# Two of four counted V chunks in plain fp32, their gate rows fetched beside the fixed chunks, and a changed pace of the list

## The chip, the cores and the metric

One core of a Trainium2 chip runs the kernel. The metric is the time of one execution in microseconds (us) of the device, as the median of several runs. A profile is one further execution with the hardware profiler on; its span runs from the first instruction to the last.

## The reference

The kernel computes one encoder layer for 256 tokens of width 2048. Most of it (retention, a gated recurrence, cross attention) isn't touched. The change lies in the last part, a layer of 16384 single-neuron experts of which each token uses 128:

```python
def block(args):                     # xb: tokens, eb: their experts, gb: gates
    xb, eb, gb = args
    u = u_tab[eb]
    act = jax.nn.gelu(jnp.einsum('td,tkd->tk', xb, u).astype(jnp.float32))
    return jnp.einsum('tk,tkd->td', (gb * act).astype(xb.dtype), v_tab[eb])
```

So for each chosen expert there is a dot product with a row of U, a gelu, a gate, and a row of V added with that weight. The result is added to the residual stream and normed.

## The kernel before

**Three ways to an expert.** The experts are arranged in 128 columns of 128. Each way computes part of them.

- *Fixed columns.* The first 40 columns are computed for all 256 tokens, used or not, in five chunks (0 to 4) of eight columns. Their U and V are loaded densely with DMAs that SP issues, 512 KB each.
- *Counted columns.* The program counts which of the other columns are used most and takes 32 of them, chunks 5 to 8. Their U and V rows are gathered by index: one indirect DMA, issued by POOL, brings the 128 rows of a column (128 x 2048 numbers). Their gates come the same way, four indirect DMAs of 128 x 256 for half a chunk.
- *The list.* What then remains of a token's experts is worked off one by one: for each of up to 38 places of a token, in two blocks of 128 tokens, a row of U is gathered for every token of the block and multiplied with its activations (`dot`, L1415), later a row of V is gathered and added with its coefficient (`axpy`, L1423). Each is one DVE instruction over 128 x 2048 and one gather by POOL (L1408).

**Products.** A product of two fp32 operands is made in three parts. ACT rounds the weight tile to a high part (`hi`, L1350), DVE subtracts to get the rest (`lo`, L1369; L1366 where the tile comes from the transposer), and PE adds activation-high x hi, activation-low x hi and activation-high x lo (L1174 to L1177 in fixed, L1187 to L1190 in counted V chunks). A V step is one half megabyte of weights and twelve matmuls of 512 columns. The activations of a chunk are split the same way, by ACT (L1293) and DVE (L1297, tile `xe`). All eight sums of V live in eight PSUM banks.

**The order.** The stretch that the change touches is written out by hand. `run` (L1316) walks through a list of steps: 64 D steps (counted U; PE first transposes each half row tile, L1339), then the V chunks in the order 0, 1, 2, 3, 5, 6, 7, 8, sixteen steps each: W steps for fixed chunks, R steps for counted ones. Between them stand G steps, which load two halves of gates and multiply them into the next chunk's activations (L1274 for fixed chunks, L1285 for counted ones). Chunk 4 comes last, in `v_final`, after the loop. At step t the loop emits the high part of step t + 3, the low part of t + 2, loads of up to step t + 8 where a buffer is free, the matmuls of t, and then `wv.pump(rate)`. The pump lets the list go on: it adds the step's rate to a credit, and each list operation takes 2.2 from it. The rates are RU = 2.3 for a D step and RV = 1.35 for a V step. What is left of the list after the loop is emitted at once (`wv.drain`), ahead of `rest`, a branch that is skipped when the list was long enough, and of `v_final`.

**The buffers.** Weight loads and gates share six tiles (`spots`), two of which are the halves of the buffer that held chunk 0's activations. Row gathers of V take `rows_v`: the buffers that held the activations of chunks 1, 2, 3 and 5, each given when its activations have been split. The list has `ring`: four tiles, and from the sixth and seventh V chunk on one more each. `chosen` (L1442) refills it before each operation, with the buffer that the operation before has just used.

**The queues.** Each engine works off its instructions in the order of the program and waits at semaphores. POOL's queue is the one to watch: row gathers, gate gathers and list gathers stand in it in the order in which the loop emitted them, and where one waits for its buffer, all behind it wait too. SP issues only the dense loads here.

Of the kernel before, what the change touches and what calls it, by code (L numbers as in the profile page):

```python
# [18 lines left out]
P = 128  # L19
# [18 lines left out]
RG, RK, RU, RV = 8.0, 3.5, 2.3, 1.35  # L38
# [46 lines left out]
def hybrid_layer_kernel(ctx: ExitStack, tc: tile.TileContext, a: dict, out: bass.AP, dbg=None):  # L85
# [1105 lines left out]

    class Step:
        def __init__(self, kind, load, mms, rate, part=0, post=None):
            self.kind, self.load, self.mms, self.rate, self.part = kind, load, mms, rate, part
            self.post = post or {}
# [44 lines left out]
    def v_steps(i):  # L1240
# [17 lines left out]
        if i < NCH:  # L1258
            for dc in range(4):
                for q in range(4):  # L1260
                    yield Step("W", lambda b, dc=dc, q=q: nc.sync.dma_start(b, a["V"][i, dc, q]),
                               lambda hi, lo, dc=dc, q=q: products(hi, lo, dc, q), RV)
        else:
            for c in range(8):
                for half in range(2):
                    yield Step("R", None if half else column(c),
                               lambda hi, lo, c=c, half=half: r_mms(*ahs[i], hi, lo, c, half), RV, half)

    def prep_steps(i, gap=2):
# [40 lines left out]
        return reads, post  # L1310
# [6 lines left out]
    spots, rows_u, rows_v = [], [], []  # L1317

    def run(steps):
# [4 lines left out]
        def loads(limit):  # L1324
            for k, q in queues.items():
                while q and q[0] <= limit and free[k]:
# [16 lines left out]
        def high(t):  # L1343
            if t < len(steps) and steps[t].kind != "G":
# [10 lines left out]
        def low(t):  # L1355
            if t >= len(steps):
                return
# [14 lines left out]
            elif kind == "R" and steps[t].part:  # L1372
                rows_v.append(raws[t])
            del raws[t]
# [9 lines left out]
        for t, step in enumerate(steps):  # L1384
# [8 lines left out]
            if step.kind != "G":  # L1393
# [46 lines left out]
    def chosen():  # L1440
# [17 lines left out]
        held, taken = [], 0  # L1458
        for kind, tt, k, gs in ops:
# [17 lines left out]
            else:  # L1477
                while "v0" not in done:
                    yield 3.0
                axpy_pe(tt, k, mine[0])  # L1480
            ring.extend(mine)
            yield 0.4 if kind == "pe" else 2.2
# [235 lines left out]
    def begin():  # L1718
# [3 lines left out]
        spots.extend(held_in[ORDER[0]][:, 1024 * n:1024 * n + 1024] for n in range(2))  # L1722
# [8 lines left out]
    def given(n):  # L1731
        (rows_v if n < 5 else ring).append(held_in[ORDER[n]])
# [3 lines left out]
    attach(steps[-1], {1: [(begin, None)]})  # L1736
    for n, (i, nxt) in enumerate(zip(ORDER[:-1], ORDER[1:])):
# [5 lines left out]
        if n + 1 < NCH + NDY - 2:  # L1743
            attach(part[-1], {1: [(lambda n=n: given(n + 1), None)]})
        for k, g in enumerate(reads):
            part.insert(2 + 5 * k, g)
        steps += part
# [97 lines left out]
```

## Time and profile before

| what | value |
|---|---|
| median of 3 runs | 2057.37 us (2057.12 to 2061.39) |
| the profiled execution's own time | 2054.45 us |
| its span | 2052.7 us |
| mean granted TensorE clock | 0.966 |
| counted U stage | about 1255 to 1532 us |
| eight V chunks in the loop | about 1532 to 1980 us |
| chunk 4, norm and output | about 1980 to 2053 us |
| PE busy in the span | 1885.0 us (92%) |
| DVE busy | 1577.2 us (77%) |
| POOL busy | 547.7 us (27%) |

PE, DVE, ACT, POOL and SP are the engines; PEld is PE's loading of stationary operands. A row of a timeline gives the start, the duration, the engine, the line of the kernel, the operation, what it writes and reads, and in brackets how long its engine stood idle before it and what ended that. A POOL row is the issue of a gather, not the transfer. Busy time is no bound by itself: a stage is bound by what ends last there.

### The profile page before, as it was taken

The page shows a single profiled execution, that of the slowest core. Times are in us where ns is not written, and L with a number is a line of the kernel's source. Part 1 is how long each engine was busy: PE and PEld are TensorE (multiplying, and loading weights), DVE is VectorE, ACT ScalarE, POOL GpSimd, SP SyncE. Part 2 cuts the span into 40 slices and gives each one's busy share as a digit, 9 for nine tenths or more (in the row PEclk, how much of TensorE's full clock was granted, in tenths as well). Part 3 has the DMA queues.
Part 4 walks back from the last instruction along what each step waited for, and adds up shares of the span by engine and source line. Part 5 has one row for each costly group of instructions (what it writes and reads, how often), then busy time and mean ns, then how long its engine had stood idle before and what let it go on. Part 6 is the DMA issues. An engine that isn't in the chain of part 4 may idle for free. (4 is left out here: it accounts for less than half of the span.)

```text
span 2052.7 us, 27876 instructions
## 1 busy us (share of the span) xinstructions
PE 1885.0 (92%) x10196; PEld 1600.4 (78%) x10196; DVE 1577.2 (77%) x2402; ACT 916.2 (45%) x1418; POOL 547.7 (27%) x371
## 2 busy tenths in 40 slices
PE   9999999999999999999888787988999888877878
PEld 8888888888889888888777666877887766655666
DVE  6868967744566558999967576987999879866886
ACT  6566444544555545554556433333333332321333
POOL 1200000000000000000155312544634357868741
PEclk9999999999999999999999889999999999988989
DMA  8775656566655468556467876998988989797973
GB/s 291 264 224 172 213 162 192 162 197 191 186 173 146 154 185 292 168 180 201 147 136 153 213 241 241 394 355 304 390 328 316 416 334 348 261 359 287 365 273 129
DMA packets 203244, 499.87 MB, mean 244 GB/s; under 512 B 106760, under 2 KB 113032, under 8 KB 174856
## 3 DMA queue, kind: packets, MB, share of 16 engines
q1 hardware_dynamic: 72288, 254.23, 38.2%
q0 software_dynamic: 36240, 228.29, 28.7%
q10 hardware_dynamic: 94576, 15.54, 4.3%
q8 instruction: 80, 1.31, 0.3%
q14 instruction: 60, 0.49, 0.1%
HBM read 503.24 MB, written 21.30 MB: 256 GB/s over the span
## 5 line engine op out<-in xcount | busy, mean ns | idle before, releaser
L133 DVE TENSOR_TENSOR lo<-raw,hi 128x1024 fp32r<-128x1024 f32 x364 | 449.3, 1237 | 206.2 <-PE xc L187 125.2
L132 ACT CAST hi<-raw 128x1024 fp32r<-128x1024 f32 x364 | 382.0, 1052 | 288.8 <-PE xc L185 171.9
L142 PE MATMUL U<-xn,hi 128*128 128x512 f32 x1152 | 312.6, 407 | 0.4 <-DVE foldu L1221 0.4
L142 PEld LDWEIGHTS U<-xn,hi 128*128 128x128 f32 x1152 | 212.1, 194 | 37.1 <-DVE foldu L1221 0.7
L1415 DVE SCALAR_TENSOR_TENSOR junk<-at,h 128x2048 bf16<-128x2048 f32 x74 | 169.1, 2285 | 28.0 <-DMA at<-in_Us_dram,idx 27.9
L1350 ACT CAST hi<-kept 128x1024 fp32r<-128x1024 f32 x83 | 83.9, 1048 | 214.7 <-DMA kept<-in_Vs_dram,dyn 139.1
L144 PEld LDWEIGHTS U<-xn,lo 128*128 128x128 f32 x1152 | 158.5, 193 | 23.9 <-DVE lo L133 12.7
L144 PE MATMUL U<-xn,lo 128*128 128x256 f32 x1152 | 164.0, 285 | 9.7 <-DVE lo L133 9.7
L780 POOL DMA_DIRECT2D hn<-h x2 | 1.1, 566 | 508.6 <-DVE h L778 508.6
L1187 PE MATMUL acc<-hi,xe 128*128 128x512 f32 x256 | 107.5, 420 | 30.0 <-ACT hi L1350 30.0
L1423 DVE SCALAR_TENSOR_TENSOR hh<-at,coef,hh 128x2048 f32<-128x2048 f32 x47 | 110.2, 2346 | 29.5 <-DMA at<-in_Vs_dram,idx 29.5
L1369 DVE TENSOR_TENSOR lo<-kept,hi 128x1024 fp32r<-128x1024 f32 x83 | 99.7, 1218 | 33.4 <-ACT hi L1350 33.4
L1408 POOL DMA_INDIRECT at<-in_Us_dram,idx x74 | 82.7, 1117 | 139.1 <-DVE junk L1415 103.6
L142 PE MATMUL wb<-hT,hi 128*128 128x512 f32 x448 | 116.9, 396 | 0.0
L1113 POOL TENSOR_TENSOR kept<-kept 128x512 f32<-128x512 bf16 x64 | 77.3, 1216 | 122.8 <-DVE kept L1112 91.7
L1188 PE MATMUL acc<-hi,xe 128*128 128x512 f32 x256 | 106.3, 415 | 0.0
L1174 PE MATMUL acc<-hi,xe 128*128 128x512 f32 x240 | 97.9, 408 | 2.9 <-ACT hi L1350 2.8
L1408 POOL DMA_INDIRECT at<-in_Vs_dram,idx x47 | 82.2, 1749 | 57.5 <-DVE hh L1423 36.2
L1175 PE MATMUL acc<-hi,xe 128*128 128x512 f32 x240 | 96.1, 400 | 0.0
L1177 PE MATMUL acc<-lo,xe 128*128 128x512 f32 x240 | 67.5, 404 | 28.7 <-DVE lo L1369 16.2
L142 PEld LDWEIGHTS wb<-hT,hi 128*128 128x128 f32 x448 | 80.6, 189 | 13.9
L1112 DVE TENSOR_TENSOR kept<-kept,kept 128x512 bf16<-128x512 bf16 x128 | 69.8, 592 | 27.3 <-POOL kept L1113 15.2
(498 smaller groups left out, 4250.6 us busy)
## 6 DMA issues: line engine op xcount, KB each, us to landing
raw<-in_U_dram SPq DMA_DIRECT2D x80, 512.0 KB, 3.7
raw<-in_V_dram SPq DMA_DIRECT2D x61, 512.0 KB, 6.9
raw<-in_w_qkv_dram SPq DMA_DIRECT2D x48, 512.0 KB, 4.2
raw<-in_w_xyg_dram SPq DMA_DIRECT2D x44, 512.0 KB, 4.4
raw<-in_w_xk_dram SPq DMA_DIRECT2D x32, 512.0 KB, 3.6
raw<-in_w_xv_dram SPq DMA_DIRECT2D x32, 512.0 KB, 3.7
raw<-in_w_out_dram SPq DMA_DIRECT2D x32, 512.0 KB, 3.6
raw<-in_w_xq_dram SPq DMA_DIRECT2D x32, 512.0 KB, 3.6
```

The lines of the kernel that those rows point to most:

```text
L132: A.copy(hi, raw)
L133: V.tensor_tensor(lo, raw, hi.bitcast(F32), op=ALU.subtract)
L142: PE.matmul(pt, hi[:, ks], xt[:, kb, :], start=(kb == 0), stop=(kb == KB - 1))
L144: PE.matmul(pt[:, :T], lo[:, ks], xt[:, kb, :T], start=False, stop=False)
L1174: PE.matmul(pt, ah[:, c, t_], hi[:, w], start=(first and c == 0), stop=False)
L1175: PE.matmul(pt, al[:, c, t_], hi[:, w], start=False, stop=False)
L1187: PE.matmul(pt, ah[:, c, t_], hi[:, w], start=False, stop=False)
L1188: PE.matmul(pt, al[:, c, t_], hi[:, w], start=False, stop=False)
L1369: V.tensor_tensor(los[t], part_of(t), his[t].bitcast(F32), op=ALU.subtract)
L1408: G.indirect_dma_start(dst, None, src, bass.IndirectOffsetOnAxis(ap=ix, axis=0), bounds_check=n - 1, oob_is_err=False)
L1415: V.scalar_tensor_tensor(junk, gat, 1.0, h[0], op0=ALU.mult, op1=ALU.mult, accum_out=coef[tt][:, k:k + 1])
L1423: V.scalar_tensor_tensor(hh[tt], gat, coef[tt][:, k:k + 1], hh[tt], op0=ALU.mult, op1=ALU.add)
```

## The change

- Counted chunks 5 and 7 (`PLAIN`) are multiplied in plain fp32: four matmuls of fp32 operands a step in place of twelve, straight from the gathered rows and from the activations in their place. Their steps have no `hi` and no `lo`, and their activations are not split. A row buffer is handed back once PE's matmuls of the column are emitted, and the activations' buffer after the chunk.
- The G steps of all four counted chunks move into the four fixed chunks, two into each, at places 12 and 15. Those of the fixed chunks stay.
- A list operation's buffer goes back to the ring one operation later, from the end of the first V chunk on.
- The pump's rates become 1.9 for a D step, 1.25 for a split V step and 3.1 for a plain one.
- Row gathers may be loaded up to four steps earlier, and `rows_v` gets the buffers of chunks 1, 2, 3, 5 and 6, and at last the two halves of chunk 0's. The ring gets those of chunks 7 and 8.
- In `loads` the limit and the loop variable now share a name, so that one call takes at most one load from a queue.

```diff
-RG, RK, RU, RV = 8.0, 3.5, 2.3, 1.35
+RG, RK, RU, RV, RP = 8.0, 3.5, 1.9, 1.25, 3.1
+PLAIN = (5, 7)
...
+    def p_mms(av, row, c, half):
+        for tt in range(TT):
+            for d in range(2):
+                dc = 2 * half + d
+                PE.matmul(acc[dc][tt], av[:, c, tt * P:(tt + 1) * P], row[:, dc * 512:(dc + 1) * 512],
+                          start=False, stop=False)
...
-        if i < NCH:
+        if i in PLAIN:
+            for c in range(8):
+                for half in range(2):
+                    yield Step("R", None if half else column(c),
+                               lambda row, c=c, half=half: p_mms(acts[i], row, c, half), RP, half, plain=True)
+        elif i < NCH:
...
-        return reads, post
+        return reads, {} if i in PLAIN else post
...
-        def loads(limit):
+        def loads(t):
             for k, q in queues.items():
-                while q and q[0] <= limit and free[k]:
+                while q and q[0] <= t + (4 if k == "R" else 0) and free[k]:
                     t = q.pop(0)
...
+            if not queues["WG"] and lent and all(any(b is f for f in spots) for b in lent):
+                spots[:] = [f for f in spots if all(b is not f for b in lent)]
+                lent.clear()
+                rows_v.append(held_in[ORDER[0]])
...
-            if step.kind != "G":
+            if step.plain:
+                step.mms(raws[t])
+                if step.part:
+                    rows_v.append(raws[t])
+                del raws[t]
+            elif step.kind != "G":
                 step.mms(his.pop(t), los.pop(t))
...
-            ring.extend(mine)
-            yield 0.4 if kind == "pe" else 2.2
+            used.append(mine)
+            if len(used) > ("v0" in done):
+                ring.extend(used.pop(0))
+            yield 0.4 if kind == "pe" else 2.2
...
-        (rows_v if n < 5 else ring).append(held_in[ORDER[n]])
+        (rows_v if n < 6 else ring).append(held_in[ORDER[n]])
...
-        if n + 1 < NCH + NDY - 2:
-            attach(part[-1], {1: [(lambda n=n: given(n + 1), None)]})
-        for k, g in enumerate(reads):
+        for m in (n, n + 1):
+            if 0 < m < NCH + NDY - 1 and m == n + (ORDER[m] not in PLAIN):
+                attach(part[-1], {1: [(lambda m=m: given(m), None)]})
+        for k, g in enumerate(reads if nxt < NCH else []):
             part.insert(2 + 5 * k, g)
+        if n < len(early_reads):
+            for k, g in enumerate(early_reads[n]):
+                part.insert(12 + 3 * k, g)
```

POOL's queue at the start of the counted V chunks, before. `kept` tiles written from `in_Vs_dram,dyn` are V rows of a counted column, `at` and `h` tiles written from `in_Vs_dram,idx` are rows of the list, and `gt` is the table of gates (four gathers in the row marked x4).

```order
L1408 DMA h_4236<-in_Vs_dram,idx 128x2048
L1254 DMA kept_7753<-in_Vs_dram,dyn 128x2048
L1408 DMA at_10566<-in_Vs_dram,idx 128x2048
L1254 DMA kept_7754<-in_Vs_dram,dyn 128x2048
L1408 DMA at_10568<-in_Vs_dram,idx 128x2048
L1279 DMA raw<-gt,dyn 128x256 x4
L1408 DMA at_10570<-in_Vs_dram,idx 128x2048
L1254 DMA kept_7752<-in_Vs_dram,dyn 128x2048
```

The same place after the change (L1431 is the list's gather, L1263 the row's, L1293 the gates'):

```order
L1263 DMA kept_7752<-in_Vs_dram,dyn 128x2048
L1263 DMA kept_7753<-in_Vs_dram,dyn 128x2048
L1263 DMA kept_7754<-in_Vs_dram,dyn 128x2048
L1293 DMA kept_7751<-gt,dyn 128x256 x4
L1431 DMA at_10566<-in_Vs_dram,idx 128x2048
L1431 DMA h_4236<-in_Vs_dram,idx 128x2048
L1431 DMA at_10568<-in_Vs_dram,idx 128x2048
L1431 DMA at_10570<-in_Vs_dram,idx 128x2048
L1431 DMA at_10566<-in_Vs_dram,idx 128x2048
L1431 DMA h_4236<-in_Vs_dram,idx 128x2048
L1431 DMA at_10568<-in_Vs_dram,idx 128x2048
L1263 DMA kept_7752<-in_Vs_dram,dyn 128x2048
```

The last four gate gathers stand here, behind three row gathers and ahead of the first plain chunk. From there on no gate gather follows in POOL's queue, and two or three list gathers stand between two rows of a plain chunk, where there was one.

DVE's queue in the middle of the counted V chunks, before: `lo` is the low part of a half row tile, `hh` the list's sum.

```order
L1369 TENSOR_TENSOR lo<-kept_7753,hi 128x1024
L1423 SCALAR_TENSOR_TENSOR hh_14553<-at_10570,coef,hh_14553 128x2048
L1369 TENSOR_TENSOR lo<-kept_7753,hi 128x1024
L1369 TENSOR_TENSOR lo<-kept_7754,hi 128x1024 x2
L1423 SCALAR_TENSOR_TENSOR hh_14553<-h_4236,coef,hh_14553 128x2048
L1285 TENSOR_TENSOR kept_7750<-raw,kept_7750 128x1024
```

After the change, where chunk 6 ends and plain chunk 7 begins (L1446 is the list's operation, L1383 the low part):

```order
L1383 TENSOR_TENSOR lo<-kept_7754,hi 128x1024
L1446 SCALAR_TENSOR_TENSOR hh_14527<-at_10566,coef,hh_14527 128x2048
L1446 SCALAR_TENSOR_TENSOR hh_14527<-h_4236,coef,hh_14527 128x2048
L1446 SCALAR_TENSOR_TENSOR hh_14527<-at_10568,coef,hh_14527 128x2048
L1446 SCALAR_TENSOR_TENSOR hh_14527<-at_10570,coef,hh_14527 128x2048
```

In a plain chunk DVE has list operations one behind the other, 21 or 22 in each, and only the split of the next chunk's activations among them. In all, the order has 65 list operations in the U stage, 79 in the V chunks and 6 behind them before, and 54, 96 and none after; the four fixed chunks have 10 each before, and 10, 8, 9 and 10 after.

More of the change, by code (lines that the diff above doesn't have):

```diff
@@ L1190, in r_mms, with __init__ @@
                         PE.matmul(pt, ah[:, c, t_], lo[:, w], start=False, stop=False)
+    def p_mms(av, row, c, half):
[4 more added lines that the diff above has]
+                          start=False, stop=False)
     class Step:
-        def __init__(self, kind, load, mms, rate, part=0, post=None):
+        def __init__(self, kind, load, mms, rate, part=0, post=None, plain=False):
+            self.plain = plain
             self.kind, self.load, self.mms, self.rate, self.part = kind, load, mms, rate, part
@@ L1316, in hybrid_layer_kernel @@
     ahs, spare = {}, {}
-    spots, rows_u, rows_v = [], [], []
+    spots, rows_u, rows_v, lent = [], [], [], []
     def run(steps):
@@ L1343, in high @@
         def high(t):
-            if t < len(steps) and steps[t].kind != "G":
+            if t < len(steps) and steps[t].kind != "G" and not steps[t].plain:
                 his[t] = ws.tile([P, 1024], F32R, tag="hi", name="hi", bufs=4)
@@ L1355, in low @@
         def low(t):
-            if t >= len(steps):
+            if t >= len(steps) or steps[t].plain:
                 return
@@ L1457, in chosen @@
         gathers = [g for o in ops for g in o[3]]
-        held, taken = [], 0
+        held, taken, used = [], 0, []
         for kind, tt, k, gs in ops:
@@ L1480, in chosen @@
                 axpy_pe(tt, k, mine[0])
+            used.append(mine)
+            if len(used) > ("v0" in done):
+                ring.extend(used.pop(0))
+            yield 0.4 if kind == "pe" else 2.2
+        for mine in used:
             ring.extend(mine)
-            yield 0.4 if kind == "pe" else 2.2
         loose = [b for b in ring if all(b is not t for t in kept)]
@@ L1721, in begin @@
         ring.append(h[1])
-        spots.extend(held_in[ORDER[0]][:, 1024 * n:1024 * n + 1024] for n in range(2))
+        lent.extend(held_in[ORDER[0]][:, 1024 * n:1024 * n + 1024] for n in range(2))
+        spots.extend(lent)
     def after_first():
@@ L1736, in hybrid_layer_kernel @@
     attach(steps[-1], {1: [(begin, None)]})
+    early_reads = [prep_steps(i)[0] for i in ORDER if i >= NCH]
     for n, (i, nxt) in enumerate(zip(ORDER[:-1], ORDER[1:])):
```

## The prediction

> **What bounds the kernel now.** I read first the busy time by stage. The cuts are the counted U stage, the eight V chunks in their order (0, 1, 2, 3, 5, 6, 7, 8) and the closing part. The columns are start and end, length, busy time and count of PE, PEld, DVE, ACT and POOL, granted clock, DMA share, GB/s.
>
> ```profile
> 1255.00:1532.00 277.00, 247.36 (x1538) 216.45 (x1537) 236.97 (x301) 94.43 (x207) 135.81 (x99) 0.96 0.91 349
> 1532.00:1583.00 51.00, 46.94 (x197) 37.39 (x196) 47.92 (x47) 20.26 (x23) 21.09 (x13) 0.97 0.84 304
> 1583.00:1634.00 51.00, 45.79 (x194) 36.78 (x193) 45.03 (x34) 17.56 (x18) 18.36 (x11) 0.97 1.01 409
> 1634.00:1682.00 48.00, 45.51 (x193) 35.17 (x192) 43.76 (x30) 20.22 (x20) 22.77 (x9) 1.00 0.94 372
> 1682.00:1741.00 59.00, 47.57 (x195) 37.72 (x194) 47.20 (x32) 16.80 (x17) 44.12 (x24) 0.91 0.86 324
> 1741.00:1795.00 54.00, 47.50 (x195) 37.27 (x194) 44.80 (x31) 18.11 (x18) 43.97 (x25) 0.94 0.74 273
> 1795.00:1859.50 64.50, 50.86 (x193) 40.01 (x192) 45.00 (x30) 17.78 (x18) 45.92 (x25) 0.84 0.86 336
> 1859.50:1925.50 66.00, 49.74 (x192) 39.59 (x192) 45.79 (x31) 17.80 (x18) 49.87 (x28) 0.87 0.84 329
> 1925.50:1979.60 54.10, 48.44 (x200) 38.50 (x198) 47.07 (x31) 19.06 (x19) 35.82 (x19) 0.94 0.82 319
> 1979.60:2052.70 73.10, 51.50 (x200) 39.25 (x200) 48.63 (x55) 22.17 (x34) 18.73 (x12) 0.88 0.48 163
> ```
>
> DVE has the same 44 to 48 us of work in every V chunk, yet a chunk takes 48 to 66 us. What differs is POOL: 9 to 13 gathers in the three short chunks, 19 to 28 in the others. The timelines of POOL and DVE inside the sixth chunk show how the two are tied (start, duration, engine, line).
>
> ```profile
> 1820.31 0.99 POOL L1254 DMA_INDIRECT kept<-in_Vs_dram,dyn  x1 [0.30 <-issue]
> ...
> 1842.68 4.23 POOL L1408 DMA_INDIRECT kept<-in_Vs_dram,idx  x1 [0.30 <-issue]
> 1847.21 5.37 POOL L1408 DMA_INDIRECT at<-in_Vs_dram,idx  x1 [0.30 <-issue]
> ```
>
> ```profile
> 1827.21 2.35 DVE L1423 SCALAR_TENSOR_TENSOR hh<-at,coef,hh 128x2048 f32<-128x2048 f32 x1 [10.67 <-DMA at<-in_Vs_dram,idx]
> ...
> 1841.42 2.35 DVE L1423 SCALAR_TENSOR_TENSOR hh<-at,coef,hh 128x2048 f32<-128x2048 f32 x1
> 1843.69 1.22 DVE L1369 TENSOR_TENSOR lo<-kept,hi 128x1024 fp32r<-128x1024 f32 x1
> 1844.82 1.22 DVE L1297 TENSOR_TENSOR xe<-kept,xe 128x1024 fp32r<-128x1024 f32 x1
> 1845.96 2.35 DVE L1423 SCALAR_TENSOR_TENSOR hh<-at,coef,hh 128x2048 f32<-128x2048 f32 x1
> ```
>
> DVE sat idle for the 10.67 us before 1827.21, and there a gather is issued in 0.99 us. With DVE backlogged the one begun at 1842.68 ends at 1846.91, 0.95 us after the list operation of 1845.96 began. So a busy DVE lets about one gather through per list operation. A chunk has 10 list operations. In the fourth to eighth chunk POOL has 14 + 15 + 15 + 18 + 9 = 71 gathers more than that, and these chunks take 297.6 us, 72.6 us over five times 45: 1.02 us for each gather in excess. That price, PE's 2.72 us a step (below) and the DMA rate are what I cost the change with.
>
> **The change part by part.** The sum is against the profiled execution (span 2052.7 us, own time 2054.45 us); its result goes on the median of the runs, 2057.37 us, which is 2.9 us above that time.
>
> *U stage.* The starts of PE's transposes, then three DVE rows, show its pace:
>
> ```profile
> 1285.60 1.04 PE L1339 MATMUL uT<-ident,row 128*128 128x128 f32 x8
> 1289.26 1.04 PE L1339 MATMUL uT<-ident,row 128*128 128x128 f32 x8
> ...
> 1434.98 1.97 PE L1339 MATMUL uT<-ident,row 128*128 128x128 f32 x8 [5.86 <-DVE lo L1366]
> ...
> 1516.78 1.04 PE L1339 MATMUL uT<-ident,row 128*128 128x128 f32 x8
> ```
>
> ```profile
> 1375.88 1.28 DVE L1366 TENSOR_TENSOR lo<-uT,hi 128x512 fp32r<-128x512 f32 x2
> 1377.08 2.28 DVE L1415 SCALAR_TENSOR_TENSOR junk<-at,h 128x2048 bf16<-128x2048 f32 x1
> ...
> 1379.29 1.28 DVE L1366 TENSOR_TENSOR lo<-uT,hi 128x512 fp32r<-128x512 f32 x2
> ```
>
> PE needs 3.66 us a step. From 1285.60 to 1516.78 lie 55 steps, 201.3 us of work in 231.2: 30 us are lost to late rows. DVE needs 1.20 + 2.21 us a step, with 65 list operations on 64 steps, and half a fold besides: hardly less than PE, so it has no reserve to catch up with. The pump of 1.9 places 54 there: 11 x 2.21 = 24 us less DVE work, 0.38 us of reserve a step. I take 18 of the 30 us; the ends are 0 (late DMA alone sets it) and 28.
>
> *Fixed V chunks (first four).* All 32 gate-row gathers now stand here. The order gives 10 + 8 + 9 + 10 list operations and 8, 8, 8 and 11 gathers beyond them (the last with three row gathers), 35, where the table has 3 + 1 - 1 + 14 = 17. 18 x 1.02 = +18 us. DVE loses three list operations (6.8 us) and two residues (2.3 us), gains six gate products (6.8 us). The wait below goes, since the second chunk now has dot products only: -5.7.
>
> ```profile
> 1598.85 2.35 DVE L1423 SCALAR_TENSOR_TENSOR hh<-h,coef,hh 128x2048 f32<-128x2048 f32 x1 [5.70 <-DMA hh<-hd]
> ```
>
> Together +10 us. Ends: -8 if DVE's gaps take all extra gathers; +25 if each of the other three chunks pays the 11 us by which the fourth now exceeds the third (33 in place of 18). The loader now takes at most one weight load a step; I cost that at nothing, since each load waits for the buffer of the load six before it in either order, and SP has little else; without that cover every load would come two steps later.
>
> *Plain chunks (5 and 7).* On PE, twelve matmuls become four. The chain of waits has two fp32 products of 512 columns (four records), and PE's timeline the step of twelve:
>
> ```profile
> 2003.81 1.72 PE acc L1616 x4
> ```
>
> ```profile
> 1913.50 1.07 PE L1190 MATMUL acc<-lo,xe 128*128 128x512 f32 x4
> 1916.22 1.07 PE L1190 MATMUL acc<-lo,xe 128*128 128x512 f32 x4
> ```
>
> 4 x 0.86 = 3.44 us against 2.72: +11.5 us of PE a chunk, 55 instead of 43.5. DVE loses 16 subtractions of 1.13 us, but the pump of 3.1 puts 22 list operations there: 22 x 2.27 = 50 us. ACT's casts go, off the path. DMA carries 8 row gathers and 22 list gathers, costed from these:
>
> ```profile
> q0 software_dynamic: 11713, 71.94, 77.4%
> ...
> kept<-in_Vs_dram,dyn POOLq DMA_INDIRECT x31
> at<-in_Vs_dram,idx POOLq DMA_INDIRECT x25
> raw<-gt,dyn POOLq DMA_INDIRECT x12
> kept<-in_Vs_dram,idx POOLq DMA_INDIRECT x10
> h<-in_Vs_dram,idx POOLq DMA_INDIRECT x8
> kept<-gt,dyn POOLq DMA_INDIRECT x8
> ```
>
> ```profile
> 1600.00:1650.00 50.00, 45.38 (x191) 36.78 (x192) 49.79 (x34) 18.73 (x18) 24.86 (x11) 0.97 1.02 415
> ```
>
> A full row gather is 128 x 8 KB = 1.05 MB, a gate gather 0.13 MB; 71.94 - 31 x 1.05 - 20 x 0.13 leaves 36.8 MB for 43 list gathers, 0.86 MB each (rows out of bounds aren't fetched). 8 x 1.05 + 22 x 0.86 = 27.3 MB, at 415 GB/s 66 us. So DMA ends last and a plain chunk takes 66 us; the ends are 57 (PE alone) and 86 (second rival). A row's buffer now comes back when PE has done its column, not when DVE has split it: POOL waits there with up to three list gathers behind, up to 6.9 us, hidden while the ring holds rows.
>
> *Chunks 6 and 8.* Their gate gathers are gone, part of their rows comes early through six row buffers. Chunk 6: DVE 16 x 1.13 + 9 x 2.27 = 38.6 and 9 gathers in excess, 47.5 us. Chunk 8, in which the list ends: 18.1 + 7 x 2.27 + 4 x 1.13 + 6 = 44.5, say 45. With the plain ones 224.5 us against 54 + 64.5 + 66 + 54.1 = 238.6: -14. Ends -36 (57 + 44 + 57 + 44) and +26.
>
> *Hand-back one operation later* costs nothing: a gather still waits for the same operation four before it, and only lets other gathers pass in POOL's queue.
>
> *The end of the list.* Six list operations now follow the last step, and PE waits for them:
>
> ```profile
> 1992.01 2.07 PE L1177 MATMUL acc<-lo,xe 128*128 128x512 f32 x4 [12.48 <-DVE lo L1590]
> ```
>
> The new order has none; a branch and a first split stay, 2.5 us: -10 (ends -6, -12.5).
>
> Sum: -18 + 10 - 14 - 10 = -32 us; 2057.4 - 32 = 2025, I say 2026 us.
>
> A rule that speaks against the middle term: the Trainium skill, "SBUF — State Buffer", section "Who interferes with whom", says that a VectorE instruction with two SBUF inputs disturbs GpSimd only where that reads SBUF, and infers that descriptor generation escapes. The trace disagrees: 0.99 us against 4.23 and 5.37 under just such instructions.
>
> **The rivals.** *POOL is not the bound.* If the gathers in excess cost nothing and the long chunks waited for DMA, the fixed chunks gain 8 us instead of losing 10, and the others come to 66 + 44 + 66 + 44 = 220, -18: -18 - 8 - 18 - 10 = -54, 2003 us. For it: in the second chunk DMA runs at 409 GB/s. Against it: the seventh is longest at 329. That page's rule would give this case.
>
> *The list starves in the plain chunks* (the slower side). Four buffers serve 22 operations there, and lists stand before the next chunk's splits on DVE. A V load lands in 10.4 us in the fixed chunks, and with list operations back to back a gather took 2.98 us to issue:
>
> ```profile
> raw<-in_V_dram SPq DMA_DIRECT2D x40, 512.0 KB, 10.4
> ```
>
> ```profile
> 1977.65 2.98 POOL L1408 DMA_INDIRECT at<-in_Vs_dram,spi  x1 [1.67 <-DVE hh L1423]
> ```
>
> (2.35 + 2.98 + 10.4) / 4 = 3.9 us an operation, 86 us a plain chunk, the four 264.5, +26: sum +8, 2065 us. It decides from 82 us a plain chunk on, a landing of 9.6 us. Against it: fewer loads are in flight there.
>
> *Given back*: late DMA alone sets the U stage (0) and the fixed chunks pay the full +25; 0 + 25 - 14 - 10 = +1, 2058 us, no change. For it: the U stage runs at 349 GB/s with a DMA share of 0.91.
>
> **How the numbers follow.** Forecast (2026, its own ends 2010 to 2042) 0.54; POOL free (2003) 0.15; list starves (2065) 0.2; given back (2058) 0.11. About 0.2%, 4 us, can be told from no change. The given-back case is worth about that much to either side: 0.08 of its chance is the same, 0.01 faster and 0.02 slower, and 0.02 of the list case ends within 4 us. So faster 0.54 + 0.15 + 0.01 = 0.7, same 0.1, slower 0.2. The range leaves out the outer half of the two extreme cases: 1998 to 2064.
>
> **What would show it.** Right: U steps near 3.66 us with under 15 us lost; the fixed chunks 215 to 225 us with POOL at 17 or more gathers; 60 to 72 us for each plain chunk at about 400 GB/s, PE issuing 3.44 us steps; no 12 us gap ahead of L1617. Wrong: a plain step far from 3.44 us, plain chunks over 80 us, fixed chunks at 200, or U still losing 30 us.

## The result and the profile after

The changed kernel takes 2038.35 us (median of 4 runs, 2037.77 to 2039.42), the kernel before 2058.97 us beside it (4 runs, 2057.12 to 2061.39). The ratio is 0.990, with a 95% interval of 0.9883 to 0.9917. The profiled execution took 2037.77 us, its span is 2036.0 us. So the time fell by some 20 us where 31 were forecast; against the profiled execution before, by 16.7 us.

The busy time by stage of the changed kernel, cut at PE's first transpose of the U stage and at the first matmul of each V chunk (0, 1, 2, 3, 5, 6, 7, 8, then the closing part). The columns are those of the table in the prediction.

```profile
1260.60:1508.20 247.60, 238.96 (x1537) 214.57 (x1538) 213.97 (x277) 92.71 (x201) 119.77 (x89) 0.99 0.91 348
1508.20:1559.30 51.10, 46.78 (x194) 36.74 (x193) 45.86 (x44) 19.65 (x23) 30.35 (x20) 0.97 1.00 394
1559.30:1616.50 57.20, 47.92 (x194) 37.56 (x193) 46.48 (x42) 18.64 (x19) 27.69 (x17) 0.91 0.88 326
1616.50:1667.20 50.70, 46.03 (x194) 36.87 (x193) 45.57 (x38) 19.69 (x20) 30.94 (x17) 0.97 0.88 321
1667.20:1723.10 55.90, 46.70 (x194) 37.83 (x193) 41.60 (x27) 14.75 (x14) 33.63 (x22) 0.91 1.00 397
1723.10:1785.90 62.80, 55.92 (x130) 23.95 (x128) 46.96 (x21) 2.19 (x3) 47.31 (x26) 1.00 0.93 355
1785.90:1848.30 62.40, 50.17 (x193) 39.23 (x194) 46.17 (x28) 16.11 (x16) 42.77 (x25) 0.86 0.87 334
1848.30:1902.80 54.50, 54.50 (x130) 24.17 (x128) 36.03 (x16) 3.04 (x3) 32.59 (x20) 1.00 0.99 388
1902.80:1976.10 73.30, 51.04 (x194) 39.95 (x193) 55.49 (x39) 23.21 (x24) 34.52 (x21) 0.84 0.78 295
1976.10:2036.00 59.90, 50.75 (x209) 38.90 (x207) 36.79 (x48) 21.49 (x34) 9.67 (x7) 0.95 0.39 134
```

To compare every kernel by the same cuts, the next table gives the stage lengths in us, read from each one's profiled execution at the starts of the same instructions. "Fixed" is the sum of chunks 0 to 3. The last column is the median of the runs; the time before in the three sets of runs was 2057.2 (first four kernels of the experiments), 2057.9 (next four) and 2059.1 (last four). One far longer run each of rows_before (2613 us), ring6 (4766 us) and the kernel before (6455 us, second set) is in these medians and in none of the ratios; without it they are 2036.92, 2030.43 and 2056.84 us.

| kernel | U | fixed | 5 | 6 | 7 | 8 | closing | median |
|---|---|---|---|---|---|---|---|---|
| before | 275.9 | 208.5 | 53.7 | 64.7 | 66.2 | 52.3 | 75.1 | 2058.97 |
| changed | 247.6 | 214.9 | 62.8 | 62.4 | 54.5 | 73.3 | 59.9 | 2038.35 |
| rows_before | 268.1 | 200.7 | 56.0 | 65.3 | 63.8 | 52.0 | 74.4 | 2038.74 |
| dve_before | 257.7 | 186.0 | 51.1 | 52.2 | 51.9 | 43.9 | 70.6 | 1977.28 |
| rows_after | 245.8 | 207.7 | 58.0 | 60.7 | 54.5 | 66.6 | 59.9 | 2015.29 |
| dve_after | 243.6 | 203.3 | 59.3 | 58.2 | 54.5 | 62.7 | 59.9 | 2003.75 |
| no_plain | 246.5 | 247.5 | 56.2 | 59.7 | 55.2 | 57.8 | 61.6 | 2045.62 |
| gates_back | 248.4 | 203.5 | 74.8 | 66.5 | 60.0 | 77.2 | 59.9 | 2046.09 |
| loads_limit | 249.1 | 219.5 | 65.6 | 61.8 | 54.5 | 70.4 | 59.9 | 2042.24 |
| gates_earlier | 247.7 | 219.3 | 62.4 | 62.4 | 54.5 | 75.9 | 59.9 | 2038.83 |
| ring6 | 247.4 | 219.1 | 61.4 | 59.9 | 59.4 | 58.1 | 59.9 | 2030.98 |
| handback_now | 246.7 | 216.1 | 63.9 | 53.4 | 54.5 | 72.2 | 59.9 | 2030.83 |
| even_pace | 247.2 | 236.2 | 54.5 | 61.9 | 54.5 | 60.4 | 61.5 | 2034.34 |
| ring6_even | 248.8 | 228.1 | 56.6 | 56.0 | 58.1 | 53.9 | 59.9 | 2025.63 |

By these cuts the change did this: U -28.3, fixed chunks +6.4, counted chunks 236.9 to 253.0, so +16.1, closing part -15.2. The U stage begins 4.2 us later than before (1260.6 against 1256.4), though nothing ahead of it was touched; in the profiles of the other kernels it begins between 1257.5 and 1261.0, so this is spread between executions. The sum is -16.8, to 0.1 the difference of the spans. Each length comes from one execution. How far such lengths scatter can be read from ring6: in chunks 0 to 3 it has the same instructions in the same order as the changed kernel, and took 219.1 us for 214.9. So a difference of some 4 us in that column tells nothing by itself.

**U stage.** The same 55 steps as in the prediction, from PE's transposes of the ninth step to those of the last, take 208.91 us. With 201.3 us of work in them 7.6 us are lost, where 29.9 were.

```profile
1284.44 1.03 PE L1353 MATMUL uT<-ident,row 128*128 128x128 f32 x8
...
1493.35 1.04 PE L1353 MATMUL uT<-ident,row 128*128 128x128 f32 x8
```

So 22.3 of the 28.3 us come from these steps. Another 5.4 come from the eight steps ahead of them (23.85 us in place of 29.24), which the prediction's count of lost time left out.

**The plain chunks and what follows them.** PE's timeline (a bracket shows idle time and what ended it) in the plain chunks and at the start of chunk 8:

```profile
1723.08 41.66 PE L1197 MATMUL acc<-kept,kept 128*128 128x512 f32 x96
...
1894.60 8.75 PE L1197 MATMUL acc<-kept,kept 128*128 128x512 f32 x20
...
1920.69 2.08 PE L1191 MATMUL acc<-lo,xe 128*128 128x512 f32 x4 [15.52 <-DVE lo L1383]
```

Eight records make a step: 41.66 / 12 = 3.47 us. PE runs through chunk 7 in 54.5 us without one stop. Then it stands for 15.52 us at the first low part of chunk 8. DVE's timeline over that time:

```profile
1905.49 1.22 DVE L1311 TENSOR_TENSOR xe<-kept,xe 128x1024 fp32r<-128x1024 f32 x1
1906.95 2.35 DVE L1446 SCALAR_TENSOR_TENSOR hh<-h,coef,hh 128x2048 f32<-128x2048 f32 x1 [0.24 <-DMA h<-in_Vs_dram,idx]
1911.92 2.35 DVE L1446 SCALAR_TENSOR_TENSOR hh<-at,coef,hh 128x2048 f32<-128x2048 f32 x1 [2.62 <-DMA at<-in_Vs_dram,idx]
1914.77 4.74 DVE L1446 SCALAR_TENSOR_TENSOR hh<-at,coef,hh 128x2048 f32<-128x2048 f32 x2 [0.49 <-DMA at<-in_Vs_dram,idx]
1919.42 1.22 DVE L1383 TENSOR_TENSOR lo<-kept,hi 128x1024 fp32r<-128x1024 f32 x1
```

DVE is still on list operations that were placed in chunk 7, and waits for their rows. Of the 43 placed in the two plain chunks, 19 begin in chunk 5 and 15 in chunk 7. The low part needs none of them; it only stands behind them. In DVE's timeline 18 intervals in chunk 5 last 3.24 us each, 14 in chunk 7 3.68 us, against 2.27 us of work.

Chunk 6 doesn't begin so. Behind chunk 5 PE stops for 3.86 us for the first high part, then for 1.10 us for the first low part. The one long stop of chunk 6, 7.64 us, begins some 30 us into it and has another cause (handback_now, below).

**Closing part.** It has no list operation before PE's work, and PE has no gap ahead of L1617. The chain of waits there names the other direction, DVE waiting for PE:

```profile
DVE lo L1617 <- PE acc L1178: 6.3, 3, 3.3
```

### The profile page after: what moved, and what is told of

The parts are those of the page before. It is cut to its first block, busy times and chain, and to the rows that moved or that the text cites. A ratio compares the mean times of both kernels' runs of the same rounds, so it can differ in the third digit from the quotient of the medians.

```text
span 2036.0 us, 27487 instructions
## 1 busy us (share of the span) xinstructions
PE 1895.3 (93%) x10068; PEld 1574.0 (77%) x10068; DVE 1539.9 (76%) x2366; ACT 882.8 (43%) x1382; POOL 520.8 (26%) x371
## 4 chain that ended last, share of the span: by engine, by line
PE 51%; DMA 15%; issue 12%; DVE 12%; POOL 6%; ACT 2%; ACTq 1%; POOLq 0%; SPq 0%; DVEq 0%
PE wb L143 10%; PE xc L186 6%; PE xc L185 6%; PE xc L188 6%; PE wb L145 5%; DMA at<-in_Us_dram,idx 4%; DMA at<-in_Vs_dram,idx 3%; DVE lo L134 3%; POOL at L1431 3%; PE U L143 3%; PE U L145 1%; DMA h<-in_Vs_dram,idx 1%; PE G L1127 1%; DMA gt<-gs 1%; PE acc L1178 1%
## 5 line engine op out<-in xcount | busy, mean ns | idle before, releaser
L1438 DVE SCALAR_TENSOR_TENSOR junk<-at,h 128x2048 bf16<-128x2048 f32 x71 | 162.3, 2286 | 19.3 <-DMA at<-in_Us_dram,idx 19.3
L1446 DVE SCALAR_TENSOR_TENSOR hh<-at,coef,hh 128x2048 f32<-128x2048 f32 x54 | 127.0, 2351 | 45.4 <-DMA at<-in_Vs_dram,idx 43.8
L1364 ACT CAST hi<-kept 128x1024 fp32r<-128x1024 f32 x52 | 53.6, 1050 | 220.5 <-DMA kept<-in_Vs_dram,dyn 138.2
L1431 POOL DMA_INDIRECT at<-in_Us_dram,idx x71 | 83.9, 1181 | 132.4 <-DVE junk L1438 100.9
L1197 PE MATMUL acc<-kept,kept 128*128 128x512 f32 x256 | 111.0, 594 | 3.0 <-DMA kept<-in_Vs_dram,dyn 3.0
L1431 POOL DMA_INDIRECT at<-in_Vs_dram,idx x54 | 100.1, 1854 | 48.9 <-DVE hh L1446 26.9
L1175 PE MATMUL acc<-hi,xe 128*128 128x512 f32 x240 | 97.4, 406 | 6.6 <-ACT hi L1364 6.6
L1197 PEld LDWEIGHTS acc<-kept,kept 128*128 128x128 f32 x256 | 48.5, 190 | 64.4 <-issue 58.5
L1176 PE MATMUL acc<-hi,xe 128*128 128x512 f32 x240 | 95.9, 400 | 0.0
L1127 PE MATMUL G<-kept,kept 128*128 128x128 f32 x512 | 73.8, 296 | 18.6 <-POOL kept L1114 10.2
L143 PE MATMUL wb<-xT,hi 128*128 128x512 f32 x352 | 89.8, 397 | 0.0
```

The costliest lines, as they stand in the source:

```text
L143: PE.matmul(pt, hi[:, ks], xt[:, kb, :], start=(kb == 0), stop=(kb == KB - 1))
L1175: PE.matmul(pt, ah[:, c, t_], hi[:, w], start=(first and c == 0), stop=False)
L1197: PE.matmul(acc[dc][tt], av[:, c, tt * P:(tt + 1) * P], row[:, dc * 512:(dc + 1) * 512], start=False, stop=False)
L1431: G.indirect_dma_start(dst, None, src, bass.IndirectOffsetOnAxis(ap=ix, axis=0), bounds_check=n - 1, oob_is_err=False)
L1438: V.scalar_tensor_tensor(junk, gat, 1.0, h[0], op0=ALU.mult, op1=ALU.mult, accum_out=coef[tt][:, k:k + 1])
L1446: V.scalar_tensor_tensor(hh[tt], gat, coef[tt][:, k:k + 1], hh[tt], op0=ALU.mult, op1=ALU.add)
```

## The experiments

The first question was what holds the list back: the bytes of its gathers, or DVE's operations with POOL's issue beside them. Two edits answer it, each made to the kernel before and to the changed one.

### Fewer rows fetched: rows_before, rows_after

```diff
-                             bounds_check=n - 1, oob_is_err=False)
+                             bounds_check=(n * 5 // 8 if n == NS else n) - 1, oob_is_err=False)
         return dst
```

> The kernel before, with a lower bound for the list's gathers: rows in the last three eighths of the U and V tables are not fetched, so that a list gather moves about 0.54 MB in place of 0.86 (this changes the result; the number of gathers and all DVE work stay). If the counted U stage is bound by DMA, its 96 MB become about 75 MB and the stage falls from 276 us to the floor of PE, 245 to 255 us; if DVE's reserve is what it lacks, as the prediction had it, the stage stays at 268 to 278 us. For the V chunks with many gathers (59, 54, 65 and 66 us): POOL as the bound says unchanged within 3 us each, DMA as the bound says 8 to 15 us less in each.

> The changed kernel with the same lower bound for the list's gathers (0.54 MB in place of 0.86; this changes the result). The two plain chunks with the split chunk behind each took 125 and 128 us. If DMA sets the pace of the list there, the 85 MB of the four chunks become about 67 and they take 200 to 215 us in all; if the turn of POOL's issue and DVE's operation sets it, they take 240 to 253 us, and PE's first wait in the last of them stays over 10 us.

### Half the width on DVE: dve_before, dve_after

```diff
-        V.scalar_tensor_tensor(junk, gat, 1.0, h[0], op0=ALU.mult, op1=ALU.mult, accum_out=coef[tt][:, k:k + 1])
+        V.scalar_tensor_tensor(junk[:, :1024], gat[:, :1024], 1.0, h[0][:, :1024], op0=ALU.mult, op1=ALU.mult,
+                               accum_out=coef[tt][:, k:k + 1])
...
-        V.scalar_tensor_tensor(hh[tt], gat, coef[tt][:, k:k + 1], hh[tt], op0=ALU.mult, op1=ALU.add)
+        V.scalar_tensor_tensor(hh[tt][:, :1024], gat[:, :1024], coef[tt][:, k:k + 1], hh[tt][:, :1024],
+                               op0=ALU.mult, op1=ALU.add)
```

> The kernel before, with every list operation on DVE over 1024 of its 2048 columns (1.2 us in place of 2.35; this leaves out half of the list's sums); all gathers stay whole. If DVE lacks reserve in the counted U stage, it falls from 276 us to 245 to 255 us; if DMA bounds it, it stays at 268 to 278 us. In the long V chunks, POOL waiting for a busy DVE says that each falls to 47 to 50 us; DMA says that they stay within 4 us.

> The changed kernel with every list operation over 1024 of its 2048 columns (this leaves out half of the list's sums); all gathers stay whole. If DVE's operations and POOL's issue beside them set the pace of the list in the plain chunks, the four counted chunks fall from 253 us to 205 to 220; if DMA sets it, they stay at 240 us or more.

The U stage and the two longest V chunks (6 and 7) of rows_before, then of dve_before, in the columns of the stage table:

```profile
1258.50:1526.60 268.10, 246.22 (x1537) 218.03 (x1538) 236.49 (x300) 94.33 (x206) 137.31 (x99) 0.96 0.85 298
1783.20:1848.50 65.30, 49.05 (x193) 37.48 (x193) 44.98 (x31) 17.90 (x18) 51.75 (x28) 0.92 0.77 293
1848.50:1912.30 63.80, 49.81 (x194) 39.30 (x193) 45.91 (x31) 17.80 (x18) 49.80 (x28) 0.87 0.76 288
```

```profile
1260.20:1517.90 257.70, 240.43 (x1537) 215.11 (x1538) 177.48 (x307) 97.78 (x208) 113.69 (x101) 0.97 0.96 380
1754.90:1807.10 52.20, 46.26 (x193) 37.45 (x192) 35.58 (x31) 16.39 (x17) 34.44 (x27) 0.93 1.00 407
1807.10:1859.00 51.90, 45.71 (x194) 37.05 (x194) 35.53 (x31) 17.81 (x18) 37.83 (x25) 0.93 1.00 409
```

*U stage before:* 7.8 us go with fewer bytes, 18.2 us with half of DVE's list work. Neither alone gets what the change got, which took away 11 operations, bytes and DVE work together: 28.3. The two edits aren't equally strong. Fewer rows took 17% of the stage's bytes away (rate times length: 79.9 MB in place of 96.8), the half width took 25% of DVE's busy time (177.5 us in place of 236.7). *Long V chunks before:* fewer bytes change chunks 6 and 7 by +0.6 and -2.4 us, half of DVE's work by -12.5 and -14.3. So DMA was not their bound. Over the whole kernel before, half-width operations are worth 80 us (ratio 0.9613, 0.9561 to 0.9664).

*Counted chunks after the change:* 253.0 fall to 239.8 with fewer rows and to 234.7 with half of DVE's work. Each helps by 13 to 18 us, and neither clears the stage. The interval in the two plain chunks falls from 3.24 and 3.68 us to no less than 3.05 to 3.26 in both. POOL's gathers in chunk 5, grouped (count, busy, mean ns of one, idle before and why), in the changed kernel, in rows_after and in dve_after:

```profile
L1431 POOL DMA_INDIRECT at<-in_Vs_dram,idx x14 | 31.3, 2236 | 9.5 <-DVE hh L1446 6.2 <-issue 3.4
```

```profile
L1431 POOL DMA_INDIRECT at<-in_Vs_dram,idx x14 | 30.4, 2172 | 4.3 <-issue 4.3
```

```profile
L1431 POOL DMA_INDIRECT at<-in_Vs_dram,idx x15 | 16.3, 1088 | 18.0 <-DVE hh L1447 13.0 <-issue 3.2 <-DMA at<-in_Vs_dram,idx 1.5
```

The issue of a gather takes 2.24 us, 2.17 with fewer bytes, and 1.09 when DVE's operation is half as long. It follows DVE, not the bytes. With half-width operations POOL waits for a free buffer instead (13.0 us behind DVE's `hh`), and DMA comes to its limit: in chunk 7 of dve_after it moves 422 GB/s with a share of 1.01, where the changed kernel has 388 and 0.99. What describes the list's pace in a plain chunk is the round trip of a buffer, divided by four buffers. The landing comes from the DMA issues of the changed kernel in chunk 5, and in chunk 7:

```profile
at<-in_Vs_dram,idx POOLq DMA_INDIRECT x14, 8.7
```

```profile
at<-in_Vs_dram,idx POOLq DMA_INDIRECT x11, 10.3
```

These are medians, and a landing is counted from the start of its issue, so the issue is in it. The means over the trips that lie wholly in a chunk, from the timelines of POOL and DVE, are these. Chunk 5 (15 trips): 8.84 us from issue to landing, 0.23 to the start of the operation, 2.35 for the operation, and 2.07 until POOL begins the next gather into the buffer, since other gathers stand ahead of it; 13.5 / 4 = 3.4 us, where the mean interval is 3.24. Chunk 7 (11 trips): 10.43 + 0.18 + 2.35 + 1.77 = 14.7, and 14.7 / 4 = 3.68, as measured. This sum says where the time of a trip goes, not which part sets it. A cheaper part helps a little, none is the bound alone.

### No plain chunk: no_plain

```diff
-RG, RK, RU, RV, RP = 8.0, 3.5, 1.9, 1.25, 3.1
-PLAIN = (5, 7)
+RG, RK, RU, RV, RP = 8.0, 3.5, 1.9, 1.65, 3.1
+PLAIN = ()
```

> The changed kernel with no plain chunk and a rate of 1.65 for every V step, which places the same 96 list operations evenly, 12 to a chunk. The theory now: in a plain chunk PE needs nothing of DVE and runs ahead, the list falls behind it, and PE pays for that at the first split of the next chunk, so that plain chunks bring little. Then even chunks of 55 to 60 us each for the four counted ones (235 in place of 253) and about 6 us more in each fixed one: 2030 to 2046 us, the same as the changed kernel within 8. The rival, that plain chunks are what saves the time: 2055 us or more.

2045.62 us, ratio 0.9943 (0.9922 to 0.9965): some 7 us slower than the changed kernel, at the edge of the first expectation. The counted chunks are 24 us shorter (228.9), the fixed ones 33 us longer (247.5). So plain chunks do save a little, against an even pace of 1.65; other paces without plain chunks were not tried. They are not faster themselves (117.3 us for the two, 111.4 split); they take list operations out of the fixed chunks. There 48 operations begin, 37 with plain chunks: 32.6 / 11 = 3.0 us for each, more than DVE's 2.27. Some 2 us of the 32.6 are the split of chunk 5's activations, which stands there too, and the lengths scatter by some 4 us.

### The gates back in the counted chunks: gates_back

```diff
-        for k, g in enumerate(reads if nxt < NCH else []):
+        for k, g in enumerate(reads):
             part.insert(2 + 5 * k, g)
-        if n < len(early_reads):
-            for k, g in enumerate(early_reads[n]):
-                part.insert(12 + 3 * k, g)
```

> The changed kernel with the gate gathers of the counted chunks back beside the counted chunks. By the price of the prediction (1.02 us for a gather in excess) the fixed chunks fall by about 10 us to 205, and the counted ones, with 24 more gathers among them, rise by about 20: 2045 to 2052 us. The rival: the counted chunks have room on POOL beside plain PE work, and the fixed chunks' gain is all that is left: 2026 to 2032 us.

2046.09 us, ratio 0.9952 (0.9923 to 0.9981), as by the price per gather. Of the 32 gate gathers the changed kernel issues all in the fixed chunks, gates_back 14 there and 18 in the counted ones. In the profiles these 18, with their products on DVE, cost 11.4 us in the fixed chunks (214.9 against 203.5) and 25.5 us in the counted ones (278.5 against 253.0): 0.6 and 1.4 us each, so the price of 1.02 lies between. The profiled execution of gates_back was its slowest, 3.9 us above the median, so these are rough. Moving the gates is a gain of some 8 us by the medians.

### The loader's limit: loads_limit

```diff
-        def loads(t):
+        def loads(limit):
...
-                while q and q[0] <= t + (4 if k == "R" else 0) and free[k]:
+                while q and q[0] <= limit + (4 if k == "R" else 0) and free[k]:
```

> The changed kernel with a limit of its own in the loader, as before, so that one call may take several loads of a queue. The prediction costed this at nothing: 2038 us within 4. The rival: the waits of ACT for dense V tiles in the second fixed chunk (6.4 us) come from loads issued late, and go: 2028 to 2033 us.

2042.24 us, ratio 0.9928 (0.9901 to 0.9955), not to be told from the changed kernel. In the second fixed chunk PE's stop for ACT is 4.32 us in place of 6.43, but the four fixed chunks take 219.5 us, so earlier loads bring nothing there. The first eight steps of the U stage take 26.95 us, where the changed kernel, and the seven other runs that keep its loader and leave rows and operations whole, take 23.3 to 24.1: the limit gains some 3 us there, which the later steps give back in part (U 249.1 against 247.6).

For the rows of counted V columns the shared name does not hold a call to one load. Once a row is taken the limit moves on with it, and the next row, two steps on, lies within the four that are added; so rows are taken as long as buffers are free.

### The gates ahead of the rows: gates_earlier

In the fourth fixed chunk of the changed kernel PE stands once, since DVE waits for gates that POOL issued from 1702.09 on, behind three row gathers (POOL, DVE and PE, each from its timeline):

```profile
1699.82 1.97 POOL L1263 DMA_INDIRECT kept<-in_Vs_dram,dyn  x1 [0.30 <-issue]
1702.09 1.97 POOL L1293 DMA_INDIRECT kept<-gt,dyn  x1 [0.30 <-issue]
...
1714.22 1.23 DVE L1299 TENSOR_TENSOR kept<-kept,kept 128x1024 f32<-128x1024 f32 x1 [9.89 <-DMA kept<-gt,dyn]
...
1716.63 2.07 PE L1178 MATMUL acc<-lo,xe 128*128 128x512 f32 x4 [9.20 <-DVE lo L1383]
```

```diff
-                part.insert(12 + 3 * k, g)
+                part.insert(6 + 3 * k, g)
```

> The changed kernel with the moved gate steps at places 6 and 9 of a fixed chunk in place of 12 and 15, so that in the fourth chunk they stand ahead of the three row gathers. If PE's wait of 9.2 us there is due to the gates standing behind three megabytes of rows, it goes and nothing replaces it: 2028 to 2032 us. The rival: gates and dense loads share six tiles, and the wait moves to another step: 2036 to 2042 us.

2038.83 us, ratio 0.9907 (0.9874 to 0.9939): no gain. The rival held. The wait at those gates is gone, but gates in the third chunk now cost PE 7.69 us, and in the fourth a list gather stands behind the rows instead (PE in the third chunk, DVE in the fourth):

```profile
1640.56 2.07 PE L1178 MATMUL acc<-lo,xe 128*128 128x512 f32 x4 [7.69 <-DVE lo L1383]
```

```profile
1717.22 2.35 DVE L1446 SCALAR_TENSOR_TENSOR hh<-at,coef,hh 128x2048 f32<-128x2048 f32 x1 [8.36 <-DMA at<-in_Vs_dram,idx]
```

### The hand-back as before: handback_now

```diff
-            if len(used) > ("v0" in done):
-                ring.extend(used.pop(0))
+            ring.extend(used.pop(0))
```

> The changed kernel with a list buffer handed back at once, as before. The prediction costed the later hand-back at nothing, since a gather waits for the same operation in either order: 2038 us within 4. The rival: that the rows of a counted column pass a list gather in POOL's queue by the later hand-back is worth something, and the time goes to 2044 us or more.

2030.83 us, ratio 0.9864 (0.984 to 0.9888): both theories fell, since it is some 7 us faster than the changed kernel (whose interval it just meets). The gain stands in one chunk, the sixth: 62.4 us against 53.4. Every list gather stands one place of the list further back in POOL's queue with the later hand-back. At this point that puts the gather for the list's fortieth V operation behind four row gathers (from 1800.99 to 1807.97), and DVE waits for it, PE for DVE (POOL, DVE and PE of the changed kernel):

```profile
1798.73 1.96 POOL L1431 DMA_INDIRECT at<-in_Vs_dram,idx  x1 [0.30 <-issue]
1800.99 0.99 POOL L1263 DMA_INDIRECT kept<-in_Vs_dram,dyn  x1 [0.30 <-DMA kept<-in_Vs_dram,dyn]
...
1807.97 1.95 POOL L1263 DMA_INDIRECT kept<-in_Vs_dram,dyn  x1 [0.30 <-issue]
1810.23 0.99 POOL L1431 DMA_INDIRECT at<-in_Vs_dram,idx  x1 [0.30 <-issue]
...
1819.52 2.35 DVE L1446 SCALAR_TENSOR_TENSOR hh<-at,coef,hh 128x2048 f32<-128x2048 f32 x1 [7.72 <-DMA at<-in_Vs_dram,idx]
...
1823.07 2.07 PE L1191 MATMUL acc<-lo,xe 128*128 128x512 f32 x4 [7.64 <-DVE lo L1383]
```

With the early hand-back the same gather is the last ahead of the four rows, issued at 1797.33, and its operation runs at 1809.91 without a wait. The one behind the rows is then the forty-first; DVE waits 3.46 us for it, PE 2.36:

```profile
1797.33 1.97 POOL L1431 DMA_INDIRECT at<-in_Vs_dram,idx  x1 [0.30 <-DVE lo L1383]
...
1809.91 2.35 DVE L1446 SCALAR_TENSOR_TENSOR hh<-at,coef,hh 128x2048 f32<-128x2048 f32 x1
...
1817.99 2.35 DVE L1446 SCALAR_TENSOR_TENSOR hh<-at,coef,hh 128x2048 f32<-128x2048 f32 x1 [3.46 <-DMA at<-in_Vs_dram,idx]
...
1821.54 2.08 PE L1191 MATMUL acc<-lo,xe 128*128 128x512 f32 x4 [2.36 <-DVE lo L1383]
```

### Another buffer for the list: ring6

```diff
-                rows_v.append(held_in[ORDER[0]])
+                ring.append(held_in[ORDER[0]])
...
-        (rows_v if n < 6 else ring).append(held_in[ORDER[n]])
+        (rows_v if n < 5 else ring).append(held_in[ORDER[n]])
```

> The changed kernel with two buffers given to the list in place of the rows: that of chunk 0's activations after the dense loads end, and that of chunk 6's. The theory: in a plain chunk the list's pace is the round trip over four buffers (landing 8.7 to 10.3 us, operation 2.3, issue about 2, so 13 to 14.6 us for four, 3.3 to 3.6 us an operation; 3.24 and 3.68 were measured). With five buffers in chunk 5 and six in chunk 7 it goes to 2.6 to 2.9, PE's first wait in chunk 8 from 15.5 us to under 6, the four counted chunks from 253 to 235 to 243 us: 2020 to 2028 us. The rivals: POOL gets hardly more than one gather through for each operation of DVE, or DMA at 355 to 390 GB/s has no room and each landing only takes longer; then the pace stays over 3.1 and the time at 2034 to 2044 us.

2030.98 us, ratio 0.9861 (0.9834 to 0.9887), between the two expectations. Its premise was half wrong: chunk 0's buffer comes free only in chunk 8, so the order has four list buffers in chunk 5 as before, and five from chunk 6 on. The interval in chunk 5 stays at 3.22 us. In chunk 7 it falls from 3.68 to 3.35, not to the 2.9 that five buffers would give at the same trip of 14.7 us. There DMA has no room: the landing grows to 12.2 us, and DMA runs at 422 GB/s with a share of 1.01 (chunk 7 of ring6, in the columns of the stage table, and its list gathers):

```profile
1846.80:1906.20 59.40, 55.36 (x129) 24.04 (x127) 42.50 (x20) 2.11 (x3) 42.07 (x25) 0.99 1.01 422
```

```profile
at<-in_Vs_dram,idx POOLq DMA_INDIRECT x12, 12.2
```

So the rival named for DMA held in that chunk, though not in the time. Chunk 7 takes 59.4 us, since PE stops at its end for 3.95 us for the first high part of chunk 8. PE's wait for the low part in chunk 8 is 3.91 us in place of 15.52, and chunks 7 and 8 take 117.5 us in place of 127.8.

```profile
1913.93 2.07 PE L1191 MATMUL acc<-lo,xe 128*128 128x512 f32 x4 [3.91 <-DVE lo L1383]
```

### A flatter pace: even_pace, and with the buffer: ring6_even

```diff
-RG, RK, RU, RV, RP = 8.0, 3.5, 1.9, 1.25, 3.1
+RG, RK, RU, RV, RP = 8.0, 3.5, 1.9, 1.45, 2.2
```

> The changed kernel with rates of 1.45 for split and 2.2 for plain V steps: 15 or 16 list operations in a plain chunk in place of 21 or 22, and about 10.5 in each split one in place of 9. If a list operation costs about the same 2.2 to 2.7 us wherever it stands (11 fewer in the counted chunks gave back 24 us there, 13 more in the fixed ones took 33, in the run without plain chunks), the counted chunks lose about 15 us, the fixed ones gain about 15: 2034 to 2042 us. The rival: the backlog that PE meets behind a plain chunk (15.5 us) is lost on top of that price, and its going is worth 10 us or more: 2022 to 2030 us.

2034.34 us, ratio 0.987 (0.9843 to 0.9896), not clearly better than the changed kernel. The counted chunks get 21.7 us shorter, the fixed ones 21.3 longer for 7 more operations, 3.0 us each again. So the backlog costs nothing on top, as far as these lengths can tell; it is list work that has to stand somewhere.

ring6_even has the edits of ring6 and these rates:

```diff
-RG, RK, RU, RV, RP = 8.0, 3.5, 1.9, 1.25, 3.1
+RG, RK, RU, RV, RP = 8.0, 3.5, 1.9, 1.35, 2.6
```

> The two buffers for the list and a middle pace (1.35 and 2.6: 18 list operations in a plain chunk). If the round trip over the buffers is what holds the list up, the two edits together leave no wait over 4 us behind a plain chunk: 2015 to 2026 us. If POOL or DMA holds it up, 2034 to 2042 us.

2025.63 us, ratio 0.984 (0.9814 to 0.9867): the fastest of the whole kernels, some 13 us under the changed one, just inside the first expectation. PE's waits of over 1 us at the start of chunk 8 are 3.04, 1.16 and 3.10. Whether the early hand-back adds to it was not tried.

## Why the prediction was right in sum, and where not

The time lies in the range and on the forecast side, 12 us above the value. By its steps, against the profiled executions:

- **U stage, -18 forecast, -28.3 measured.** The mechanism held, DVE without reserve; half-width operations alone give 18.2, though they shorten POOL's issues too. In the 55 steps that were counted the gain is 22.3; the 5.4 in the steps ahead of them were not in the sum. That the eleven operations also take their bytes away, which rows_before puts at up to 7.8, may be why the 18 were too few; this was not tried by itself. DVE and late DMA both held the stage up, where the prediction let each be an end of the range.
- **Fixed chunks, +10 forecast, +6.4 measured.** The 18 gathers cost 11.4 with their products (gates_back), 0.6 us each, not 1.02; that DVE's gaps take the rest is likely, not shown. The other 5 that come back (203.5 against 208.5) are hardly more than the scatter of 4. The length of 214.9 us lies at the edge of the 215 to 225 that was named.
- **Counted chunks, -14 forecast, +16.1 measured: the step that failed.** It laid all list operations into the chunk in which the order places them, and let DMA end a plain chunk at 66 us. DMA's rate was nearly right (355 and 388 GB/s, share 0.93 and 0.99), but in a plain chunk PE doesn't wait for the list. It ran chunk 7 at its own floor, 54.5 us, and left the list behind; chunk 8 paid, 73.3 us where 45 were forecast. Chunk 6 took 62.4 for 47.5, but 9.0 of that are the hand-back of the next point. The counted chunks took 253.0 us, nearer to the 264.5 of the rival in which the list starves than to the 224.5 of the forecast: its interval over four buffers, 3.9 us, was measured as 3.24 and 3.68. Only its place was another, not the plain chunk but PE's first low part behind it.
- **Hand-back later, nothing forecast, about 7 us of loss measured (within the +16.1 above).** The step named the passing of other gathers in POOL's queue and gave it no price. That passing was the price: rows went ahead of a list gather, and DVE, which serves both, stood for the list.
- **End of the list, -10 forecast, -15.2 measured** for the whole closing part; the gap of 12.48 us is gone.
- **Loader's limit, nothing**: borne out by loads_limit for the whole time.

The misses against -32: -10 in U, -4 in the fixed chunks, -5 at the end, +30 in the counted chunks, +4 of spread ahead of the stage; together +15, which is the difference to -17. The total came near through errors of both signs; that is luck.

**The rivals.** That the long chunks waited for DMA and not for POOL falls for the kernel before: with fewer bytes chunks 6 and 7 stay as they are, with shorter DVE operations they get 12.5 and 14.3 us shorter, and the issue of a gather in the changed kernel halves with DVE's operation. The half width shortens DVE's own work as well (45.2 to 35.6 us busy in chunk 6), so it doesn't part the two; but in chunk 7 of the kernel before DVE stood idle for 20 of 66.2 us, 14.5 of them for high parts that ACT could not make before the rows came. The Trainium skill, "SBUF — State Buffer", section "Who interferes with whom", infers that descriptor generation is not disturbed by a VectorE instruction with two SBUF inputs; the runs show 2.24 us beside the full operation and 1.09 beside the half one, and the measurement decides. But these gathers read their row numbers from SBUF, and the section's other rule, that such an instruction disturbs GpSimd where that reads SBUF, may cover them; no run here parts the two. "Given back" fell with the U stage.

What stays open: in the plain chunks no part of the round trip could be singled out with four buffers, the shares of DVE and DMA in the U stage come from one profiled execution of each kernel, and what chunk 6 lost beyond the hand-back (53.4 us for the 47.5 forecast) was not traced to a cause.

## What to carry to other kernels

When an engine is freed from waiting for a queue, look for its next wait on that queue: work placed beside it may not get done there, and is then met later, in front of the first instruction that does need the queue (15.5 us in chunk 8). Price a side stream by its round trip (issue to landing, operation, and the wait until the next gather may begin) over its number of buffers, check that the queue's rate has room for it, and place no more of it in a stage than that allows. A reordering in a shared queue is never free by its dependencies alone; ask what now stands ahead of the transfer that is needed first.

## What the hardware showed

The matmuls behind a long stop are slower. In chunk 8 of the changed kernel four records took 2.08 us right behind the 15.52 us of idle, and 1.07 us once PE had run on without a stop; this row is from the same timeline:

```profile
1943.31 1.07 PE L1191 MATMUL acc<-lo,xe 128*128 128x512 f32 x4
```

In the stage tables the granted clock is 1.00 in the plain chunks and 0.84 to 0.86 in the split ones behind them, where PE is busy 50 to 51 us for twelve-matmul steps that need 43.5. The Trainium skill, "TensorE: Matmul & The Clock Gate", section "Part 1: The HAM clock gate", says that the array falls to half its clock after an idle window of some 3.4 us; the trace agrees on the half clock, with 2.08 us against 1.07, but not on the window as a limit, since in the same chunk four records took 2.07 us also behind stops of 2.36 and 3.01 us. So a stop costs more than its length: of chunk 8's 29.8 us over 43.5, 22 are idle and 7.5 are slower matmuls.
